# A hybrid decoder layer on one core: the first unit of the merge taken into the last chain of gated linear attention, that branch's constants loaded later, and the last stores issued from two queues

## The chip, the cores and the metric

The kernel runs on one core of one Trainium2 chip. The metric is the device time of one execution in microseconds (us); lower is better. Three runs of the kernel before were timed, and one more execution was profiled.

## What is computed

One layer for 2048 new tokens and 8 x 8 sample tokens, all in f32. The reference, cut to what matters:

```python
z = jnp.einsum('btd,dn->btn', x, w_in)               # all input projections
o_att = swa(q, k, v)                                  # sliding-window attention
o_gla, S = gla(gq, gk, gv, log_a, s0)                 # gated linear attention (GLA), 4 heads
h_att = einsum(o_att * silu(g_att), w_pa)             # merge: four products ...
h_gla = einsum(o_gla * silu(g_gla), w_pg)
merged = sigmoid(x @ w_ra) * h_att + sigmoid(x @ w_rg) * h_gla
x = layer_norm(DN_ALPHA * x + merged @ w_o, ln_g, ln_b)
```

## The kernel before

All large products run on TensorE with each f32 operand split in a high and a low half: `split` (L114) lets ScalarE (ACT) cast the high half and VectorE (DVE) subtract for the low one, and each product takes three matmuls (hi x hi, hi x lo, lo x hi). TensorE's order is the order of the code. The instructions of ACT, DVE, GpSimd (POOL) and SyncE (SP, the main DMA queue) are put in order by a scheduler when the kernel is built; on the chip each of these engines takes its list strictly in order, and an instruction that waits holds all behind it.

The work goes through four stages. Stage 1 is attention, over six chunks of tokens (the loop `for c, (t0, T) in enumerate(CHUNKS)`). Stage 2 is GLA, four heads times six chunks. The parts of a chunk that follow on each other (`gla_a`, `gla_b`, `gla_norm`, `gla_c`, `gla_store`) are put into a list of steps by `chain` (L870), and `tick` runs one step between two projections, so that their matmuls stand between the projections'. In the last chunk of the last head the chain starts before the two gate projections, and what is left of it after them is run by `drain` (L995), with no projection between. The last step holds the transposition of the sample rows (`gla_c(B, "s", ...)`, L781) and the two stores of the gated rows to DRAM (`gla_store`, L788). In the last chunk these go through POOL's queue, behind the state's store (L881) and the two stores of sample states (L842).

Stage 3 is the merge: four passes (`w_pa`, `w_ra`, `w_rg`, `w_pg`) of seven products each (`ORDER`, Strassen-Winograd), each over three ranges of tokens: 84 units. A unit splits one tile of x (`make_x`, from `raw_x` L1045), and for four column groups p = 0..3 runs its matmuls (L1232 to L1234) into one PSUM tile and empties it (`combine`). In the first pass a unit has 4 x 6 = 24 matmuls. Its first product (i = 1) is emptied by a plain copy on ACT into a tile `a12` (L1072). The weights come through `raw_w` (L1014, tag "ws", 11 slots) and x through tag "xc" (5 slots).

Between stages 2 and 3 the memory of stage 2 is closed and given to stage 3's tiles. A new tile waits only for the old ones that it lies upon. The first `a12` tile lies upon one of the two rows of gates that the last `gla_store` writes out: its first copy waits, in both kernels, for that store's semaphore (DMASW5, which reaches the value waited for with the last store on POOL's queue).

Stage 4 is the output projection and the layer norm (`Rows`, L1260). The last tile has 64 rows (32 of each half), is normed in two halves of columns, and is stored by four DMAs from SP (L1300).

At the start SP loads the first weights and x in pieces, and POOL issues seven loads of constants that only GLA reads (L259), one of 192 KB among them.

Of the kernel before, what the change touches and what calls it, by code (L numbers as in the profile page):

```python
# [13 lines left out]
F32R = mybir.dt.float32r  # L14
# [37 lines left out]
def kernel(ctx, tc, io):  # L52
# [45 lines left out]
    def at(d, fn):  # L98

        while len(side) <= d:  # L100
            side.append([])
        side[d].append(fn)
# [61 lines left out]
    def fetch_x(src, t0, T):  # L164

        return [fetch(src, k, t0, T, unit if k < KT // 2 else xstage) for k in range(KT)]
# [87 lines left out]
    wgv = wg[:, :KT * 16].rearrange("p (k r) -> p k r", r=16)  # L254
    nc.scalar.copy(wgs[:, :, 0:16], wgv)
    nc.vector.tensor_tensor(wgs[:, :, 16:32], wgv, wgs[:, :, 0:16].bitcast(F32), ALU.subtract)
    for t, n in ((cmask, "c_causal"), (smask, "c_scausal"), (bsel, "c_bsel"), (rmask, "c_reset"),
                 (smaskr, "c_sreset"), (nw_h, "norm_w"), (bgk, "b_gk")):
        nc.gpsimd.dma_start(t, io[n])  # L259
    nc.vector.tensor_scalar(nw_h, nw_h, 0.5, None, op0=ALU.mult)  # L260
    nc.gpsimd.memset(mhalf, -0.5)
    for t in a_per + [as_per]:
        nc.gpsimd.memset(t, 0.0)
# [289 lines left out]
    for c, (t0, T) in enumerate(CHUNKS):  # L553
# [42 lines left out]

        step(lambda ps: nc.scalar.copy(vT[:, :T], ps), wt1("v"))
        at(1, vtrans)
        if c == 0:
            setup0()  # L600
            at(1, setup1)
            at(2, setup2)
            at(4, setup3)
# [266 lines left out]
    def chain(B):  # L870
# [18 lines left out]
        else:  # L889
            at(7 if short else 6, lambda B=B: gla_store(B))  # L890

    for h in range(GH):
        W2 = {}
        wcap(16 + 6 * h)
        for c, (t0, T) in enumerate(CHUNKS):
            last = c == len(CHUNKS) - 1
            Tp = T - (NS if last else 0)
            nt = Tp // P
            if c == len(CHUNKS) - 3:
                wcap(min(22 + 6 * h, 34))  # L900
            B = dict(h=h, t0=t0, T=T, Tp=Tp, nt=nt, last=last, wgk=R["wgk"], gin=gin, gv=[], sg=[])

            def wt2(*key):
                if c == 0:
                    W2[key] = wget()
                return W2[key]

            gla_z(B)
            sums = [combine_load(lambda n: wtile(name=n)) for _ in range(2 if c in (1, 2, 3) else 0)]

            def combine():
                if sums:
                    with tc.issue_after(pin["d"].ins):
                        combine_do(*sums.pop(0), nc.vector)

            wv = [wt2("v", 0), wt2("v", 1)]
            for i in range((T + P - 1) // P):
                n = min(P, T - i * P)
                ps = pd()
                if n == P:  # L920
                    proj_t(ps[:, :HV], x, i * P, n, wv, HV)
                    v = ps[:, :HV]
                else:
                    v = unit(name="vs")[:n, :HV]
                    proj_s(ps[:, :HV], v, x, i * P, wv, HV)
                    nc.vector.tensor_tensor(v, v, ps[:n, :HV], ALU.add)
                if i % 2 == 0:
                    gvt = wtile(F32R, "gv").rearrange("p (a b v) -> p a b v", a=2, b=2)
                gh, gl = gvt[:, i % 2, 0], gvt[:, i % 2, 1]
                split(gh[:n], gl[:n], v)  # L930
                if n == NS:
                    nc.scalar.copy(gh[NS:], v)
                    nc.vector.tensor_tensor(gl[NS:], v, gh[:NS].bitcast(F32), ALU.subtract)
                B["gv"].append((gh, gl))
                if last and i < 2:
                    wload()
                tick()
            end = last and h == GH - 1
            xf = None if end else fetch_x(io["xT"], *CHUNKS[(c + 1) % len(CHUNKS)])
            ps = pd()  # L940
            proj(ps[:, :T], wt2("k"), x, T)
            gla_k(B, ps[:, :T])
            combine()
            if len(CHUNKS) - 4 < c < len(CHUNKS) - 1:
                wload()
            tick()
            if not last:
                gin = gate_in(h, c + 1)
            elif h + 1 < GH:
                gin = gate_in(h + 1, 0)  # L950
            ps = pd()
            proj(ps[:, :T], wt2("q"), x, T)
            gla_q(B, ps[:, :T])
            tick()
            combine()
            if end:
                chain(B)
            for m in range(2):
                sg = unit(name="sg")
                B["sg"].append(sg)  # L960
                w = wt2("g", m)
                if m == 0 and not end:
                    xn = part_x(xf, samples=(c + 1 == len(CHUNKS) - 1))
                ps = pd()
                proj(ps[:, :T], w, x, T, mid=end)
                gate(sg, ps[:, :T], T)
                if len(CHUNKS) - 4 < c < len(CHUNKS) - 1 and m == 1:
                    wload()
                tick()
            if not end:  # L970
                chain(B)
            x = xn
# [6 lines left out]

    drain()
    phase.close()
    keep, phase, right = ExitStack(), ExitStack(), ExitStack()
    mo = keep.enter_context(tc.tile_pool(name="mo", bufs=1, side="left", reuse_waits="tile"))
# [207 lines left out]
    for tag, n, bufs in (("a12", T, 12), ("fin", T, 6), ("xc", 2 * T, 5), ("ws", KT // 2 * P, 11), ("top", 640, 1),  # L1193
# [1 line left out]
                         ("a21", T, 12), ("cs", 2 * T, 4), ("xh", KT // 2 * T, 2), ("xl", KT // 2 * T, 2),  # L1195
                         ("wh", KT // 2 * P, 8), ("wl", KT // 2 * P, 8)):
        mtile(tag, n, bufs, F32R if tag[1] in "hl" else F32)
    issue_x(0)
    issue_w(-1)
    issue_x(1)  # L1200
    issue_x(2)
    make_x(0)
    make_w(-1)
    issue_w(0)
    wo = []
    for n, (q, i, s) in enumerate(units):
# [12 lines left out]
        issue_w(n + 1)  # L1219
        make_x(n + 1)  # L1220
        make_w(n)
        xh, xl = xp.pop(n)
        for p in range(NP4):
            g = n * NP4 + p
            for j in range(g, g + 4):
                if j not in parts:
                    issue_parts(j)
            wh, wl = wts[n - s, p]
            ps = pa()[:, :T]
            for k in range(q.kh):  # L1230
                ks, ts = slice(k * P, (k + 1) * P), slice(k * T, (k + 1) * T)
                mm(ps, wh[:, ks], xh[:, ts], start=(k == 0), stop=False)  # L1232
                mm(ps, wh[:, ks], xl[:, ts], start=False, stop=False)  # L1233
                mm(ps, wl[:, ks], xh[:, ts], start=False, stop=(k == q.kh - 1))  # L1234
            q.combine(i, p, s, ps, parts.get(g))
            if n == len(units) - 1:
                if p < 3:
                    xr0.append(load_xr(runs(1, p * P, P)))
                x += [part(f, onew) for f in xf[2 * p:2 * p + 2]]
# [20 lines left out]
    class Rows:  # L1260
# [26 lines left out]
        def norm(self):  # L1287
# [6 lines left out]
            for i in range(D // N):  # L1294
                cs = slice(i * N, (i + 1) * N)
                nc.vector.scalar_tensor_tensor(z[:n, cs], z[:n, cs], mv[:n, 0:1], lng[:n, cs],
                                               ALU.subtract, ALU.mult)
                nc.vector.scalar_tensor_tensor(z[:n, cs], z[:n, cs], rs[:n], lnb[:n, cs], ALU.mult, ALU.add)
                for r, o, m in self.runs:
                    nc.sync.dma_start(io["o_y"][r:r + m, cs], z[o:o + m, cs])  # L1300

    HT = NT // 2
    order = [(t, u, n) for t in (1, 0) for u, n in ((0, TM), (TM, TM), (2 * TM, 2 * P))]
# [135 lines left out]
```

## Time and profile before

| what | value |
|---|---|
| three runs | 1843.16, 1848.11, 1849.0 us (median 1848.11) |
| the profiled execution's own time | 1846.22 us |
| its span (first to last instruction) | 1844.4 us |
| TensorE busy | 1807.9 us, 98% of the span |
| DVE, ACT, POOL busy | 69%, 46%, 23% |
| mean granted TensorE clock | 0.992 |

In the profile PE is TensorE's matmuls, PEld its weight loads, SPq and POOLq the issue of DMAs on those queues. A row of a timeline has the start, the time from the first to the end of the last instruction of the row, the engine, the line, the operation with out<-in, how many there are, and in brackets the idle time of the engine before it and what ended it. In a table of stages each engine's busy time stands with its count of instructions, and PEclk is the granted clock (1.00 is full speed).

### The profile page before, as it was taken

What the parts mean: (1) busy time and instruction counts of PE and PEld (TensorE: products, weight loads), DVE (VectorE), ACT (ScalarE), POOL (GpSimd) and SP (SyncE); (2) the same over time, 40 slices, a digit from 0 to 9 for tenths busy, and PEclk for the clock granted to TensorE, in tenths of its full rate; (3) what the DMA queues carried; (4) which work ended last, traced back from release to release, by engine and by line L of the source; (5) the groups of instructions that cost most, each with busy time, mean ns of one, the idle gap of its engine ahead of it and who ended that gap; (6) DMA issues with size and microseconds to landing.
All of it is one profiled execution on the core that took longest, in us unless ns stands there. A gap on an engine that the chain in (4) does not pass through costs nothing.

```text
span 1844.4 us, 32399 instructions
## 1 busy us (share of the span) xinstructions
PE 1807.9 (98%) x11683; PEld 1722.2 (93%) x11683; DVE 1280.9 (69%) x2662; ACT 849.9 (46%) x1947; POOL 422.3 (23%) x559
## 2 busy tenths in 40 slices
PE   8999999999999999999999999999999999989997
PEld 7998988899999999999999999999999999988886
DVE  5677778767776776777667669648657566966655
ACT  5444545645665565656546453435443543211110
POOL 3310111300110111011110243430355153631111
PEclk9999999999999999999999999999999999999998
DMA  7211013534345444543543189858887967895531
GB/s 233 63 56 38 12 47 100 165 131 156 120 148 170 143 143 144 186 132 107 181 145 119 58 274 315 283 178 292 276 311 256 310 216 245 287 312 177 166 111 41
DMA packets 199554, 315.84 MB, mean 171 GB/s; under 512 B 21453, under 2 KB 161189, under 8 KB 199376
## 3 DMA queue, kind: packets, MB, share of 16 engines
q1 hardware_dynamic: 192624, 304.61, 50.5%
q0 software_dynamic: 5616, 7.58, 1.5%
q8 instruction: 92, 1.51, 0.3%
q10 hardware_dynamic: 1152, 1.57, 0.3%
q14 instruction: 70, 0.57, 0.1%
HBM read 228.52 MB, written 86.14 MB: 171 GB/s over the span
## 4 chain that ended last, share of the span: by engine, by line
PE 91%; DVE 3%; DMA 3%; issue 1%; POOL 1%; SPq 0%; ACT 0%; DVEq 0%; ACTq 0%; POOLq 0%
PE pd L185 11%; PE pd L187 11%; PE pd L186 11%; PE pa L1234 9%; PE pa L1233 9%; PE pa L1232 9%; PE pd L199 7%; PE pd L198 7%; PE pd L200 7%; PE pa L421 2%; DMA cs<-tt_d 1%; PE pa L406 1%; PE pa L755 1%; PE pa L753 1%; PE pa L754 1%
## 5 line engine op out<-in xcount | busy, mean ns | idle before, releaser
L185 PE MATMUL pd<-x,wh 128*128 128x384 f32 (+2 forms) x1248 | 409.1, 328 | 7.0 <-ACT x L115 6.3
L186 PE MATMUL pd<-x,wh 128*128 128x384 f32 (+2 forms) x1248 | 403.5, 323 | 0.6 <-DVE x L116 0.3
L187 PE MATMUL pd<-x,wl 128*128 128x384 f32 (+2 forms) x1248 | 403.1, 323 | 0.6 <-DVE wl L116 0.6
L1233 PE MATMUL pa<-xl,wh 128*128 128x352 f32 x1176 | 381.3, 324 | 7.9 <-DVE xl L116 7.6
L1232 PE MATMUL pa<-xh,wh 128*128 128x352 f32 x1176 | 381.4, 324 | 2.6 <-ACT xh L115 2.3
L1234 PE MATMUL pa<-xh,wl 128*128 128x352 f32 x1176 | 381.9, 325 | 0.0
L185 PEld LDWEIGHTS pd<-x,wh 128*128 128x128 f32 x1248 | 236.5, 190 | 17.2 <-issue 8.9
L186 PEld LDWEIGHTS pd<-x,wh 128*128 128x128 f32 x1248 | 236.5, 190 | 2.0 <-DVE x L116 1.5
L187 PEld LDWEIGHTS pd<-x,wl 128*128 128x128 f32 x1248 | 236.1, 189 | 1.0 <-DVE wl L116 1.0
L1233 PEld LDWEIGHTS pa<-xl,wh 128*128 128x128 f32 x1176 | 222.7, 189 | 10.4 <-DVE xl L116 10.1
L1232 PEld LDWEIGHTS pa<-xh,wh 128*128 128x128 f32 x1176 | 222.5, 189 | 3.6 <-ACT xh L115 2.6
L1234 PEld LDWEIGHTS pa<-xh,wl 128*128 128x128 f32 x1176 | 224.5, 191 | 0.0
L116 DVE TENSOR_TENSOR xl<-xs,xh 128x1408 fp32r<-128x1408 f32 x63 | 110.5, 1753 | 69.4 <-ACT xh L115 35.7
L198 PE MATMUL pd<-wh,x 128*128 128x256 f32 x512 | 147.9, 289 | 0.0
L199 PE MATMUL pd<-wh,x 128*128 128x256 f32 x512 | 145.6, 284 | 1.2 <-DVE x L116 1.1
L200 PE MATMUL pd<-wl,x 128*128 128x256 f32 x512 | 144.6, 282 | 0.0
L115 ACT CAST x<-xst 128x384 fp32r<-128x384 f32 (+2 forms) x164 | 78.2, 485 | 139.9 <-PE pd L199 117.9
L115 ACT CAST xh<-xs 128x1408 fp32r<-128x1408 f32 x63 | 86.5, 1372 | 103.9 <-PE pa L1234 81.7
L746 POOL TENSOR_SCALAR sq<-sq 128x1 f32<-128x1 f32 (+1 forms) x68 | 21.4, 314 | 467.2 <-ACT ring L745 467.2
L199 PE MATMUL pd<-woh,x 128*128 128x512 f32 x256 | 101.5, 396 | 0.0
L198 PE MATMUL pd<-woh,x 128*128 128x512 f32 x256 | 101.5, 396 | 0.0
L200 PE MATMUL pd<-wol,x 128*128 128x512 f32 x256 | 101.5, 396 | 0.0
(318 smaller groups left out, 3683.6 us busy)
## 6 DMA issues: line engine op xcount, KB each, us to landing
wst<-wt SPq DMA_DIRECT2D x33, 512.0 KB, 3.6
xs<-xc_d SPq DMA_DIRECT2D x24, 704.0 KB, 5.6
cs<-tt_d SPq DMA_DIRECT2D x48, 352.0 KB, 4.7
u<-xT SPq DMA_DIRECT2D x84, 192.0 KB, 4.0
xst<-xT SPq DMA_DIRECT2D x76, 192.0 KB, 2.6
xs<-xT SPq DMA_DIRECT2D x18, 704.0 KB, 5.9
ws<-w_ra SPq DMA_DIRECT2D x36, 256.0 KB, 4.4
ws<-w_rg SPq DMA_DIRECT2D x36, 256.0 KB, 5.6
```

The lines of the kernel that those rows point to most:

```text
L115: pin["a"] = nc.scalar.copy(dst_h, src)
L116: i = eng.tensor_tensor(dst_l, src, dst_h.bitcast(F32), ALU.subtract)
L185: mm(ps, hi[:, s], xh[:, :T], start=(k == 0), stop=False)
L186: mm(ps, hi[:, s], xl[:, :T], start=False, stop=False)
L187: mm(ps, lo[:, s], xh[:, :T], start=False, stop=(k == n - 1))
L198: mm(ps, xh[:, xs], hi, start=(k == 0), stop=False)
L199: mm(ps, xl[:, xs], hi, start=False, stop=False)
L200: mm(ps, xh[:, xs], lo, start=False, stop=(k == KT - 1))
L421: mm(ot[pr, :], vb[:, pr], A["pT", bi, kv][:, hf], start=(hf == h0), stop=(hf == 1))
L1232: mm(ps, wh[:, ks], xh[:, ts], start=(k == 0), stop=False)
L1233: mm(ps, wh[:, ks], xl[:, ts], start=False, stop=False)
L1234: mm(ps, wl[:, ks], xh[:, ts], start=False, stop=(k == q.kh - 1))
```

## The change

Three edits.

1. The first unit of the merge (pass `w_pa`, i = 1, first range: 24 matmuls) is no longer run by the merge loop. `early_load` loads its x (352 KB) and all its weights (512 KB, one tile) before the k projection of the last chunk; `early_split` splits them after the q projection; `early_product(p)` runs the six matmuls of one column group. Group 0 stands after the last gate projection, group 1 after all steps of the chain but the last, groups 2 and 3 after the last step. They are written to two kinds of PSUM tiles (`pd` for 0 to 2, `pa` for 3). The merge loop then loads no x for unit 0, runs no matmul for it, and only empties the four tiles (`combine`, the copies into `a12`).
2. The seven constants of GLA and the multiplication of `nw_h` come in the third chunk of attention, on POOL behind a copy of that chunk.
3. Of the last tile's four stores, two are issued by ACT.

```diff
+    def gla_constants():
+        for t, n in ((cmask, "c_causal"), (smask, "c_scausal"), (bsel, "c_bsel"), (rmask, "c_reset"),
+                     (smaskr, "c_sreset"), (nw_h, "norm_w"), (bgk, "b_gk")):
+            nc.gpsimd.dma_start(t, io[n])
+        nc.vector.tensor_scalar(nw_h, nw_h, 0.5, None, op0=ALU.mult)
...
+        if c == 2:
+            with tc.issue_after(pin["k"].ins):
+                gla_constants()
...
+    def early_load():
+        r = [wtile(name=n) for n in ("mx", "mw")]
+        nc.sync.dma_start(r[0][:, :2 * MT].rearrange("p (k t) -> p k t", k=2), ua_d[:, :2, :MT])
+        nc.sync.dma_start(r[1].rearrange("q (p c) -> q p c", p=4), io["w_pa"][0, 0].rearrange("p q c -> q p c"))
+        early["raw"] = r
+
+    def early_split():
+        for n_, r, w_ in zip("xw", early.pop("raw"), (2 * MT, D)):
+            hl = wtile(F32R, "mh"), wtile(F32R, "ml")
+            split(hl[0][:, :w_], hl[1][:, :w_], r[:, :w_])
+            early[n_] = hl
+
+    def early_product(p):
+        ps = early[p] = (pd if p < 3 else pa)()[:, :MT]
+        (xh, xl), (wh, wl) = early["x"], early["w"]
+        for k in range(2):
+            ks, ts = slice((2 * p + k) * P, (2 * p + k + 1) * P), slice(k * MT, (k + 1) * MT)
+            mm(ps, wh[:, ks], xh[:, ts], start=(k == 0), stop=False)
+            mm(ps, wh[:, ks], xl[:, ts], start=False, stop=False)
+            mm(ps, wl[:, ks], xh[:, ts], start=False, stop=(k == 1))
...
+            if end:
+                early_load()
...
             if end:
+                early_split()
                 chain(B)
...
+                if end and m == 1:
+                    early_product(0)
                 tick()
...
+    while len(side) > 1:
+        tick()
+    early_product(1)
     drain()
+    early_product(2)
+    early_product(3)
...
-    issue_x(0)
+    issue_x(1)
     issue_w(-1)
-    issue_x(1)
     issue_x(2)
-    make_x(0)
...
-            ps = pa()[:, :T]
-            for k in range(q.kh):
+            ps = pa()[:, :T] if n else early.pop(p)
+            for k in range(q.kh if n else 0):
...
-                for r, o, m in self.runs:
-                    nc.sync.dma_start(io["o_y"][r:r + m, cs], z[o:o + m, cs])
+                for j, (r, o, m) in enumerate(self.runs):
+                    (nc.scalar if self.end and j else nc.sync).dma_start(io["o_y"][r:r + m, cs], z[o:o + m, cs])
```

What this does to the engines' lists is seen at three places. Line numbers of the changed kernel differ from those of before (L1112 is the copy that was L1072, L754 was L748, L787 was L781; L918 to L920 are the early products' matmuls).

The first place is TensorE's list at the end of the chain. Before, from the transpositions of the last block (128 wide) and of the sample rows (64 wide) into unit 0:

```order
L837 MATMUL pa<-gv,kz 128x256
L781 MATMUL pa<-ident,ring 128x128 x2
L781 MATMUL pa<-ident,ring 128x64 x2
L1232 MATMUL pa<-xh,wh 128x352
L1233 MATMUL pa<-xl,wh 128x352
L1234 MATMUL pa<-xh,wl 128x352
```

The same place in the changed kernel, to the first product after the last transposition:

```order
L843 MATMUL pa<-gv,kz 128x256
L787 MATMUL pa<-ident,ring 128x128 x2
L918 MATMUL pd<-mh 128x352
L919 MATMUL pd<-ml,mh 128x352
L920 MATMUL pd<-mh,ml 128x352
L918 MATMUL pd<-mh 128x352
L919 MATMUL pd<-ml,mh 128x352
L920 MATMUL pd<-mh,ml 128x352
L787 MATMUL pa<-ident,ring 128x64 x2
L918 MATMUL pd<-mh 128x352
L919 MATMUL pd<-ml,mh 128x352
```

Group 1 stands behind the 128-wide transpositions and ahead of the 64-wide ones; groups 2 and 3 follow, and then unit 1.

The second place is ACT's list from the last step of the norm of the sample rows into the merge; xh and wh are the high halves of x and of the weights, "a" is the tile a12, and the brackets name the semaphores that an instruction waits for. Before:

```order
L748 ACTIVATE ring<-pa,sq 64x256 [waits Activation_49,Pool_49]
L115 CAST xh<-xc 128x704 [waits DMAHW2_49]
L115 CAST wh<-ws 128x256 [waits DMAHW3_49]
L115 CAST wh<-ws 128x256 [waits DMAHW4_49]
L115 CAST wh<-ws 128x256 [waits DMAHW5_49,PE_49]
L115 CAST wh<-ws 128x256 [waits DMAHW6_49]
L115 CAST xh<-xc 128x704 [waits DMAHW7_49]
L1072 COPY a_13651<-pa 128x352 [waits DMASW2_49,DMASW5_49,DVE_49,PE_49]
```

In the changed kernel:

```order
L754 ACTIVATE ring<-pa,sq 64x256 [waits Activation_49,Pool_49]
L1112 COPY a_13678<-pd 128x352 [waits DMASW5_49,DMASW2_49,DVE_49]
L1112 COPY a_13680<-pd 128x352 [waits DMAHW7_49,PE_49]
L1112 COPY a_13682<-pd 128x352 [waits PE_49]
L1112 COPY a_13684<-pa 128x352 [waits PE_49]
L115 CAST xh<-xc 128x704 [waits DMAHW4_49]
L115 CAST wh<-ws 128x256 [waits DMAHW5_49]
L115 CAST wh<-ws 128x256 [waits DMAHW6_49]
L115 CAST wh<-ws 128x256 [waits DMAHW7_49]
```

The four copies of unit 0 have moved from behind the casts of units 0 and 1 to the front of them; the wait for DMASW5 moved with the first.

The third place is SP's list at the same join. In the changed kernel:

```order
L904 DMA mw<-w_pa 128x4x256
L794 DMA ug_d<-sg 128x256 x2
L1085 DMA xc<-ua_d 128x2x352
L1054 DMA ws<-w_pa 128x256 x4
L1085 DMA xc<-ua_d 128x2x352
L1054 DMA ws<-w_pa 128x256 x2
L1085 DMA xc<-ua_d 128x2x352
L1054 DMA ws<-w_pa 128x256
L1085 DMA xc<-ua_d 128x2x352
L1054 DMA ws<-w_pa 128x256
L1085 DMA xc<-ua_d 128x2x352
L1054 DMA ws<-w_pa 128x256 x4
```

The early loads stand before the last stores of the chunk before (L794); five loads of x (units 1 to 5) and eleven of weights fill all slots, and of the last row's four loads of weights the fourth is the first that waits for a slot.

More of the change, by code (lines that the diff above doesn't have):

```diff
@@ L256 @@
     nc.vector.tensor_tensor(wgs[:, :, 16:32], wgv, wgs[:, :, 0:16].bitcast(F32), ALU.subtract)
[L257 to L260, printed above, removed]
+    def gla_constants():
[3 more added lines that the diff above has]
+        nc.vector.tensor_scalar(nw_h, nw_h, 0.5, None, op0=ALU.mult)
     nc.gpsimd.memset(mhalf, -0.5)
@@ L890, in chain @@
             at(7 if short else 6, lambda B=B: gla_store(B))
+    early = {}
+    def early_load():
[16 more added lines that the diff above has]
+            mm(ps, wl[:, ks], xh[:, ts], start=False, stop=(k == 1))
     for h in range(GH):
@@ L1221 @@
         make_w(n)
-        xh, xl = xp.pop(n)
+        xh, xl = xp.pop(n) if n else (None, None)
         for p in range(NP4):
```

## The prediction

> **What bounds the kernel now.** I read the page first, then the table of what TensorE waited for, the table of stages, and then the timelines of the stages in which it waits.
>
> ```profile
> PE 1807.9 (98%) x11683; PEld 1722.2 (93%) x11683; DVE 1280.9 (69%) x2662; ACT 849.9 (46%) x1947; POOL 422.3 (23%) x559
> PE pa L1233 <- DVE xl L116: 7.6, 5, 2.6
> core 0: us, PE busy (x) PEld busy (x) DVE busy (x) ACT busy (x) POOL busy (x), PEclk, DMA share, GB/s
> 0.00:30.00 30.00, 22.21 (x105) 19.61 (x106) 17.70 (x29) 17.00 (x29) 8.36 (x25) 1.00 0.61 190
> 1052.60:1064.00 11.40, 7.65 (x51) 5.45 (x52) 7.26 (x20) 5.29 (x15) 4.95 (x9) 0.93 0.96 314
> 1831.90:1844.40 12.50, 0.00 (x0) 0.00 (x0) 4.64 (x10) 0.37 (x1) 0.92 (x1) 0.58 0.08 22
> ```
>
> TensorE is busy in 1807.9 of 1844.4 us, so the kernel is as long as TensorE's list plus the 36.5 us in which it waits. Three stages hold most of those: 7.8 us in the first 30, 3.75 us at the join of GLA and merge (11.40 less 7.65), and the 12.5 us after its last matmul. The change works on these three. At the join, TensorE's timeline shows each wait (the row of 7.6 us in five waits above has the last of them), and the table of stages the clock:
>
> ```profile
> 1053.49 0.38 PE L753 MATMUL pa<-st,qih 128*128 128x256 f32 x1 [0.89 <-ACT st L115]
> 1060.71 0.70 PE L781 MATMUL pa<-ident,ring 128*128 128x128 f32 x4 [0.98 <-ACT ring L748]
> 1061.69 0.43 PE L1232 MATMUL pa<-xh,wh 128*128 128x352 f32 x1 [0.27 <-ACT wh L115]
> 1063.54 0.66 PE L1233 MATMUL pa<-xl,wh 128*128 128x352 f32 x1 [1.43 <-DVE xl L116]
> 1064.63 0.49 PE L1233 MATMUL pa<-xl,wh 128*128 128x352 f32 x1
> 1064.92 0.49 PE L1234 MATMUL pa<-xh,wl 128*128 128x352 f32 x1
> 1069.97 0.32 PE L1232 MATMUL pa<-xh,wh 128*128 128x352 f32 x1
> 1070.13 0.32 PE L1233 MATMUL pa<-xl,wh 128*128 128x352 f32 x1
> 1062.47:1069.29 6.82, 5.75 (x19) 5.70 (x20) 3.16 (x8) 0.76 (x2) 1.46 (x3) 0.50 1.03 360
> 1069.29:1076.00 6.71, 6.71 (x43) 6.71 (x43) 4.30 (x6) 6.02 (x17) 2.94 (x3) 1.00 0.48 155
> ```
>
> The waits are 0.89, 0.98, 0.27 and 1.43 us. The last two rows show a second cost: with these waits the clock is granted at 0.50 for 6.82 us. Matmuls of 352 columns start every 0.29 us there (1064.63 to 1064.92) and every 0.16 us at full clock (1069.97 to 1070.13). Unit 1 begins at 1069.97.
>
> **The change: the last stores.** SP's timeline, then the issues of that line and their landing:
>
> ```profile
> 1836.17 1.74 SPq L1300 DMA_DIRECT2D o_y<-z  x4
> L1300 SPq DMA_DIRECT2D o_y<-z x4: 331/385/429, 1836.2 to 1837.5; - x4
> DMA to landing us min/median/max: 1.6/1.7/1.7
> ```
>
> Four issues of about 0.4 us end at 1837.9, the last starting at 1837.5 and the third some 0.45 us before it, behind the second half of z. With two queues the last pair starts together at about 1837.0: -0.45 us, between -0.6 and 0 (if an issue on ACT is slower than on SP).
>
> **The constants.** Rows of ACT, TensorE, the stage from 5 to 11 us, two of the seven loads, and POOL in the third chunk:
>
> ```profile
> 13.83 1.05 ACT L115 CAST wh<-wst 128x1024 fp32r<-128x1024 f32 x1 [0.82 <-DMA wst<-wt]
> 14.93 0.44 PE L185 MATMUL pd<-x,wh 128*128 128x384 f32 x1 [0.66 <-ACT wh L115]
> 5.00:11.00 6.00, 4.77 (x12) 3.64 (x13) 3.50 (x8) 3.21 (x8) 4.35 (x14) 1.00 0.98 312
> rmask<-c_reset POOLq DMA_DIRECT2D x1, 192.0 KB, 5.3
> cmask<-c_causal POOLq DMA_DIRECT2D x1, 64.0 KB, 3.3
> 127.74 1.17 POOL L352 CAST win<-kl 128x128 fp32r<-128x128 f32 x2
> 137.99 0.29 POOL L353 CAST win<-kl 128x128 fp32r<-128x128 f32 x1 [9.08 <-DVE kl L343]
> ```
>
> From 5 to 11 us the DMA engines are full (0.98, 312 GB/s), and TensorE waits at 14.93 for weights that landed at 13.83. The seven constants, 311 KB of which these two rows are 256, take 1.0 us of that rate. I take -0.8 us; bounds -1.0 and 0, if the weights are held by SP's order instead. In the third chunk POOL issues them behind the copies that end at 128.9 and ahead of the one at 137.99, before which it waits 9.08 us for DVE. Seven issues at 0.55 us (two gates' stores take 1.09 in the next fence) end at 132.8 and delay nothing; the product with `nw_h` on DVE stands later still, behind the chunk's first scores. That costs 0.
>
> **The early unit.** Its 24 matmuls are moved, none is added. ACT's, DVE's, SP's and POOL's rows at the join, and the time to landing of POOL's last stores (first one alone, then both):
>
> ```profile
> 1028.70 23.87 SPq L788 DMA_DIRECT2D ug_d<-sg  x4
> 1041.92 0.49 DVE L724 SCALAR_TENSOR_TENSOR dm<-pd,dm 128x320 f32<-128x320 f32 x1 [2.37 <-PE pd L187]
> 1042.78 0.41 ACT L115 CAST qih<-gb 128x256 fp32r<-128x256 f32 x1 [2.30 <-DVE gb L724]
> 1060.56 0.77 ACT L115 CAST xh<-xc 128x704 fp32r<-128x704 f32 x1
> 1061.23 1.32 ACT L115 CAST wh<-ws 128x256 fp32r<-128x256 f32 x4
> 1069.98 0.45 ACT L1072 COPY a<-pa 128x352 f32<-128x352 f32 x1 [6.75 <-PE pa L1233]
> 1073.61 1.20 ACT L1072 COPY a<-pa 128x352 f32<-128x352 f32 x3
> 1062.61 0.88 DVE L116 TENSOR_TENSOR xl<-xc,xh 128x704 fp32r<-128x704 f32 x1
> 1063.94 1.14 SPq L1014 DMA_DIRECT2D ws<-w_pa  x1
> 1060.43 0.86 POOL L842 DMA_DIRECT2D o_ss<-S  x1 [0.27 <-DMA ws<-w_pa]
> 1062.84 1.09 POOL L788 DMA_DIRECT2D ug_d<-sg  x2
> ug_d<-sg POOLq DMA_DIRECT2D x1, 160.0 KB, 5.0
> ug_d<-sg POOLq DMA_DIRECT2D x2, 160.0 KB, 5.8
> ```
>
> The added splits take 0.77 and 0.88 us (x) and 1.05 and, scaled from 0.88 by 1024/704, 1.3 us (weights). They stand where ACT waits 2.30 us for DVE and DVE 2.37 us for TensorE; their loads go out on SP after the second of the four stores from 1028.70, some 8 us ahead. I take 0, at most +0.7 us, if the weights' subtraction pushes `dm` back.
>
> Group 0 (6 x 0.16 = 1.0 us) fills the 0.89 us wait: cost 0. Group 1 doesn't fill the 0.98 us: it stands behind the 128-wide transpositions, and these are what waits at 1060.71, because the PSUM tile they write is the one that the norm of the sample rows is still read from. So that gap stays; group 1 follows from 1061.05 to 1062.05, then the sample transpositions, and groups 2 and 3 end at about 1064.3 (later if the clock drops again at 1062.47; what comes after doesn't depend on it).
>
> What comes after is unit 1, and it needs ACT's cast of its x. On this step the forecast rests. Before, the first copy into `a12` comes at 1069.98, after ACT stood still for 6.75 us. The row blames TensorE, but unit 0's first product was complete when its sixth matmul ended, at 1065.4. The built program has the copy wait for the last store on POOL's queue. That one is the second of the two in the 1062.84 row, issued at 1063.38; 5.0 us for the first and 5.8 as the middle of both make 6.5 for it: it lands at 1069.9, just when the copy runs. Before, this cost nothing: ACT had cast x and weights of units 0 and 1 ahead of the copy, and TensorE had unit 0 to work on. In the changed kernel the four copies stand ahead of all these casts. Queued behind the waiting copy is the x of unit 1, and TensorE, with nothing else left, waits for that.
>
> When does the store land now? Its source is ready after the sample transpositions, some 0.4 us later; POOL is busy until then with the stores ahead of it, so the issue stays at 1063.4. Ahead of it lie the same two stores of 512 KB. SP has sent eleven loads of weights by then, not eight (0.4 MB more), and sends none of those that went out from 1063.94 on (some 0.5 MB). I take 1069.4. The lower bound is 1066.7: from 1061.3, the end of the first store's issue, 1.38 MB at the 360 GB/s of this stage (3.8 us), and 1.6 us, the shortest landing above. The upper is 1070.2, 0.3 later than before.
>
> From landing to unit 1's second matmul: 0.1 to the first copy, 4 copies at 0.37 (three took 1.20), 0.77 for xh, 0.88 for xl and 0.1 between them make 3.3 us. So this matmul comes at 1072.7 where it came at 1070.13: +2.6 us, between -0.1 and +3.4. TensorE has been idle from 1064.3 then, over 7 us, and starts slow. An event of 6.82 us at half clock costs 3.4 us if matmuls fill it, 1.7 if half of it falls in the wait; I take 2.5. (Before, unit 0 ran in such an event; that is contained in the 1070.13 from which I count.) The Trainium skill ("TensorE: Matmul & The Clock Gate", Part 1) has the clock return after some 3.4 us of sustained work; by that the loss would be 1.7 us, and the sum 0.8 us less. The event in the trace is twice as long.
>
> The early unit in all: +2.6 + 2.5 = **+5.1 us**, between +1.6 and +6.8 (+0.7 more if the splits delay).
>
> **Sum.** +5.1 - 0.8 - 0.45 = +3.85 us on the profiled execution's 1846.2, so 1850.1. The median of the runs, 1848.1, is 1.9 above that execution; on its scale the forecast is **1852.0 us**, +0.2%. Its own bounds are 1848.1 (+1.6 - 1.0 - 0.6) to 1855.6 (+6.8 + 0.7).
>
> **Rivals**, on the same scale.
>
> *The gaps are filled and ACT isn't held* (chance 0.10). If the store landed by 1064.3, the last copy would end at 1064.75, a little after group 3, and unit 1's second matmul come at 1064.75 + 0.77 + 0.88 = 1066.4: -3.7 us, of which up to 2.5 is lost again to the clock. With the other edits that is -5.0 to -2.5: 1843.1 to 1845.6. Against it stand 5.0 and 6.5 us of landing; for it, that no row of the profile names the store as what the copy waited for.
>
> *The store lands early* (0.07). The two took long because they stood behind 1 MB. If the queue is emptied sooner, the landing comes 1.7 us (as for the last stores) and 0.3 us for the data after the issue's end at 1063.9: 1065.9. Unit 1's second matmul is then at 1069.2, -0.9; the wait of some 4 us still drops the clock, +1.7; with the rest -0.45: 1847.7. The Trainium skill ("DMA: Bandwidth & Descriptors", Anatomy of one DMA) has a transfer take 2.0 us plus its bytes at 436 GB/s, 2.4 us for 160 KB, which speaks for this. Both stores in the trace took twice as long.
>
> *The weights fall behind, and it is clearly slower* (0.20).
>
> ```profile
> 1096.46 1.26 POOL L1024 TENSOR_TENSOR ws<-ws 128x256 f32<-128x256 f32 x1
> ```
>
> Slots of "ws" come free when DVE has split unit 1's weights. The load that went out at 1063.94 now waits until about 1073, 9 us later, while TensorE's need of it moves by 5.1. The weights that POOL combines lose 4 us of slack; the last of product 6 are combined until 1097.7 (the row), for matmuls near 1104. If less than 4 us is there, TensorE stops in units 6 to 11; the price is up to 4.0: +5.1 + 4.0 - 1.25 = +7.9, 1856.0. For it speaks how close that row is to its use, with a cast and a subtraction still between; against it, that this is one place in many, and later loads wait for TensorE's own pace.
>
> The rest, 0.05, is a half-clock event more or fewer elsewhere (3.4 us each).
>
> **How the numbers follow.** The forecast has 0.58. About 0.3% (5.5 us) is what a measurement of this kernel tells from no change: 1842.6 to 1853.7. Faster than that needs the first rival at its end and an event fewer: 0.05. Slower: the third rival, and the upper part of the forecast's own range: 0.28. Within: 0.67. The range of 1845.5 to 1857.0 holds the forecast's bounds and the second and third rivals, and leaves out most of the first.
>
> **What would show it.** In the changed kernel's profile: ACT idle for some 8 us before the first L1112, which starts within 0.2 us of the last gate store's landing; then four copies, xh, and TensorE's first L1271 about 3.2 us after that start, following an idle of over 6 us; the 0.98 us before L787 unchanged; no wait at group 0; at the start, the second projection's first matmul about 0.8 us earlier. I am wrong if L1112 begins by 1066, or if TensorE waits less than 4 us between its last early product and unit 1.

## The result and the profile after

| | median us | runs | lowest to highest |
|---|---|---|---|
| before | 1847.57 | 10 | 1840.9 to 1849.49 |
| changed | 1855.26 | 10 | 1847.99 to 1859.46 |

The ratio is 1.0048, with a 95% interval of 1.0031 to 1.0064: the changed kernel is slower by 0.48%, some 8.9 us. The forecast was 1852.0 us, +3.85, and a range of 1845.5 to 1857.0, so sign and range held and the size was under half of what came. The range held at its upper side: the bounds that the forecast works out for itself end at +7.5 us, and the time is nearer to the third rival's 1856.0 than to the forecast. A time above 1853.7 had been given a chance of 0.28, against 0.67 for one that can't be told from no change. One execution of all those timed for this document, among the twelve of e7 below, took 4105 us and is left out of its ratio. The profiled execution of the changed kernel is the quickest of its ten: 1847.99 us, with a span of 1846.2, 1.8 above that of before.

The step on which the forecast rested is in this trace as it was forecast, within 0.7 us. ScalarE's timeline at the join (start, duration, line, and in brackets the idle time ahead and what ended it):

```profile
1052.42 0.43 ACT L220 ACTIVATE th<-pd 128x320 f32<-128x320 f32 x1
1059.92 0.47 ACT L754 ACTIVATE ring<-pa,sq 64x256 f32<-64x256 f32 x1 [0.98 <-POOL sq L753]
1070.06 1.16 ACT L1112 COPY a<-pd 128x352 f32<-128x352 f32 x3 [9.67 <-DMA ug_d<-sg]
1071.09 0.48 ACT L1112 COPY a<-pa 128x352 f32<-128x352 f32 x1
1071.43 0.81 ACT L115 CAST xh<-xc 128x704 fp32r<-128x704 f32 x1
```

ScalarE stands still for 9.67 us, and the profile now names what it waited for, the store of the gates (`ug_d<-sg`). Before, the row of this copy blamed TensorE. Behind it come the four copies, and only then the cast of unit 1's x. POOL's issue of the two stores, and their landing from the answer on the tile `sg`:

```profile
1062.73 1.09 POOL L794 DMA_DIRECT2D ug_d<-sg  x2 [0.16 <-DVE sg L790]
DMA to landing us min/median/max: 6.7/6.8/6.8
```

The second store lands at 1069.95, 0.1 us ahead of the copy. TensorE's timeline at the same place, and the table of stages around the half clock:

```profile
1053.76 0.39 PE L760 MATMUL pa<-st,qih 128*128 128x256 f32 x1 [0.18 <-DVE st L116]
1060.44 0.44 PE L787 MATMUL pa<-ident,ring 128*128 128x128 f32 x2 [1.00 <-ACT ring L754]
1063.92 0.32 PE L920 MATMUL pa<-mh,ml 128*128 128x352 f32 x1
1072.60 0.66 PE L1270 MATMUL pa<-xh,wh 128*128 128x352 f32 x1 [8.37 <-ACT wh L115]
1073.22 0.66 PE L1271 MATMUL pa<-xl,wh 128*128 128x352 f32 x1
core 0: us, PE busy (x) PEld busy (x) DVE busy (x) ACT busy (x) POOL busy (x), PEclk, DMA share, GB/s
1067.09:1077.33 10.24, 4.73 (x15) 4.34 (x16) 4.15 (x8) 5.58 (x14) 0.96 (x2) 0.50 0.28 91
1077.33:1084.00 6.67, 6.67 (x44) 6.67 (x43) 2.44 (x5) 4.89 (x13) 0.74 (x1) 1.00 0.23 72
```

The 0.89 us wait ahead of group 0's place is gone, the wait ahead of the 128-wide transpositions is still 1.00 us, the last early product begins at 1063.92, and then TensorE has nothing to do for 8.37 us. When unit 1 comes, the clock is at 0.50 until 1077.33. Unit 2 begins 26.46 us after ScalarE's last tanh of a gate (the 1052.42 row), and in the kernel before 21.13 us after it (that tanh is at 1052.71 there): the join costs **+5.3 us**, where +5.1 was forecast.

The other two edits gave nothing. At the start, TensorE's and ScalarE's rows of before, then of after:

```profile
28.46 0.49 PE L594 MATMUL pa<-ident,vT 128*128 128x128 f32 x3
28.79 1.05 ACT L115 CAST wh<-wst 128x1024 fp32r<-128x1024 f32 x1 [2.23 <-DMA wst<-wt]
31.41 0.51 PE L301 MATMUL pa<-oh,rbh 33*128 33x384 f32 x1 [0.84 <-ACT brow L306]
```

```profile
27.41 0.49 PE L597 MATMUL pa<-ident,vT 128*128 128x128 f32 x3
28.91 1.05 ACT L115 CAST wh<-wst 128x1024 fp32r<-128x1024 f32 x1 [2.72 <-DMA wst<-wt]
31.51 0.44 PE L304 MATMUL pa<-oh,rbh 33*128 33x384 f32 x1 [2.00 <-ACT brow L309]
```

TensorE is 1.05 us ahead at the transposition of vT, but the next weights land no earlier (the cast that waits for them is at 28.91, and was at 28.79), the copies of the bias rows stand behind that cast on ScalarE, and TensorE waits 2.00 us for them where it waited 0.84.

At the end, the instructions of the last line (the program's close), before and after:

```profile
L1425 POOLq DRAIN  x3: 46/106/9372, 1834.3 to 1844.2; - x3
L1425 SPq DRAIN  x3: 7/7/7, 1839.3 to 1843.9; - x3
```

```profile
L1463 POOLq DRAIN  x3: 46/98/9371, 1836.0 to 1845.9; - x3
L1463 SPq DRAIN  x3: 7/7/7, 1840.7 to 1845.7; - x3
1836.07 0.92 POOL L1330 TENSOR_TENSOR rs<-rs,mhalf 64x1 f32<-64x1 f32 x1 [6.47 <-DVE rs L1329]
1837.94 1.03 ACTq L1338 DMA_DIRECT2D o_y<-z  x2
```

In the kernel before, VectorE's last addition into `rs` is at 1834.0 and SP is through with the last landing at 1839.3, 5.3 us later; in the changed kernel these are 1835.8 and 1840.7, 4.9 us apart: the last store did land 0.44 us sooner. But POOL's last instruction is followed by a drain of 9.37 us, and the program ends 0.8 us behind that in both kernels: 10.43 us from the addition to the end, with one queue or two. The rows of before showed this already.

### The profile page after: what moved, and what is told of

It reads as the page before. It is cut to its first block, busy times and chain, and to the rows that moved or that the text cites. A ratio compares the mean times of both kernels' runs of the same rounds, so it can differ in the third digit from the quotient of the medians.

```text
span 1846.2 us, 32397 instructions
## 1 busy us (share of the span) xinstructions
PE 1805.9 (98%) x11683; PEld 1719.1 (93%) x11683; DVE 1277.0 (69%) x2663; ACT 851.6 (46%) x1948; POOL 421.4 (23%) x559
## 4 chain that ended last, share of the span: by engine, by line
PE 89%; DVE 4%; DMA 3%; ACT 1%; issue 1%; POOL 1%; SPq 0%; DVEq 0%; ACTq 0%; POOLq 0%
PE pd L185 10%; PE pd L187 10%; PE pd L186 10%; PE pa L1271 8%; PE pa L1270 8%; PE pa L1272 8%; PE pd L199 7%; PE pd L200 7%; PE pd L198 7%; PE pa L424 2%; DMA cs<-tt_d 1%; PE pa L409 1%; PE pa L760 1%; PE pa L761 1%; PE pa L759 1%
## 5 line engine op out<-in xcount | busy, mean ns | idle before, releaser
L1271 PE MATMUL pa<-xl,wh 128*128 128x352 f32 x1168 | 377.0, 323 | 6.3 <-DVE xl L116 6.1
L1272 PE MATMUL pa<-xh,wl 128*128 128x352 f32 x1168 | 376.2, 322 | 0.0
L1272 PEld LDWEIGHTS pa<-xh,wl 128*128 128x128 f32 x1168 | 220.1, 188 | 0.1
```

## The experiments

One theory: ScalarE's queue stands behind a copy whose memory the last store still reads, and this hold is the cost. Its rivals: that the price lies elsewhere (constants, stores, weights), that other waits would take the hold's place, or that it is the waiting itself and not the queue behind it. All runs were timed beside the kernel before on the same chip. "Below" and "above" are against it.

**e1 and e10, the early unit alone** (constants and stores as before), and **e9, the changed kernel again** beside e10.

> The changed kernel with the constants and the last stores as before: the early unit alone. Theory (ScalarE is held until the last gate store lands): ScalarE idle for 8 to 10 us before the first copy of unit 0, TensorE idle for about 8.4 us before unit 1, then half clock; matmuls of unit 2 and after stand about 5.3 us later than in the kernel before, and the time is 0.2 to 0.5% above it (+4 to +9 us), most of what the whole change costs. Rival (the cost lies in the other two edits, or in the weights behind): within 0.1% of the kernel before.

> The changed kernel once more, beside e10 and e11 on one chip. The first timing gave 0.48% (0.31 to 0.64) above the kernel before, the early unit alone 0.30% (0.17 to 0.44). Theory (the early unit's hold is the whole cost, 5.3 us in the trace, and the other two edits are worth nothing): 0.2 to 0.4% above the kernel before, and within 0.1% of e10. Rival (constants and stores add to it): 0.45% or more, and over 0.15% above e10.

> The early unit alone once more, as in e1: 0.2 to 0.4% above the kernel before by the theory, and the same as e9; by the rival 0.15% or more below e9.

e1 gave 1.0030 (1.0017 to 1.0044), e10 1.0039 (1.0024 to 1.0054), e9 1.0043 (1.0027 to 1.0059). e9 is a little above the 0.2 to 0.4% that was expected, and it is 0.04% from e10. The early unit alone and the whole change differ by less than the intervals: the unit is the cost. Rows of ScalarE and TensorE in e1:

```profile
1067.38 1.16 ACT L1106 COPY a<-pd 128x352 f32<-128x352 f32 x3 [8.45 <-DMA ug_d<-sg]
1069.93 0.66 PE L1264 MATMUL pa<-xh,wh 128*128 128x352 f32 x1 [7.16 <-ACT wh L115]
```

**e2, the constants alone.**

> The kernel before with GLA's constants loaded in the third chunk, nothing else. Theory from the two traces (the microsecond gained in the first 28 us is given back at the next weights, which land no earlier): TensorE reaches the first products with the identity about 1 us earlier, waits about 1.2 us longer at the bias products near 31 us, and everything from 40 us on stands within 0.3 us of the kernel before; the time is unchanged within 0.15%. Rival (the gain of 0.8 us of the prediction holds): all from 40 us on 0.8 us earlier.

1.0002 (0.9987 to 1.0016): no change, but the interval is some 2.5 us to either side, so the time alone can't tell 0.8 us from nothing, and the rows have to. TensorE reaches the identity products at 27.51 (27.41 in the changed kernel, 28.46 before), and waits 1.47 us for the bias rows (0.84 before). One number of the theory missed: the trace stood not within 0.3 us of before from 40 us on but 1.2 us later. In it the half clock that follows these waits lasts 10.24 us, and 6.83 before (rows of before, then of e2):

```profile
31.64:38.47 6.83, 6.83 (x22) 5.86 (x22) 5.70 (x11) 3.00 (x5) 1.44 (x3) 0.50 0.87 297
```

```profile
31.09:41.33 10.24, 10.24 (x31) 9.35 (x32) 5.90 (x11) 3.14 (x5) 4.18 (x8) 0.50 0.90 281
```

TensorE's 120th matmul is still 0.2 us ahead of before, and its 150th, behind the stretch, is 1.2 us late. The other traces with the constants moved have 3.41 or 6.83 us here. The last tanh of the gates lies between 1049.6 and 1053.4 in the fourteen profiled executions, with both settings of the constants at either end, so a single trace can't show an edit of this size in this stage.

**e11, the last stores from two queues alone.**

> The kernel before with the last stores from two queues, nothing else. Theory (POOL's drain of 9.37 us ends last): the last store lands about 0.44 us sooner after the last rows' statistics, POOL's drain ends where it did, and the span's end stands 10.4 us after the last addition to the variance, as in the kernel before; the time is the same within 0.15%. Rival (the prediction's -0.45 us holds): 9.9 us.

1.0005 (0.9990 to 1.0020), too wide an interval for 0.45 us; the rows have 10.43 us from the addition into `rs` to the end, as by the theory, though the last store lands 0.3 us sooner.

**e3, the same order of work, other memory under the copies.** Two entries of the list that lays out the merge's tiles are swapped, so that `a12` lies where no late store reads:

```diff
-    for tag, n, bufs in (("a12", T, 12), ("fin", T, 6), ("xc", 2 * T, 5), ...
+    for tag, n, bufs in (("fin", T, 6), ("a12", T, 12), ("xc", 2 * T, 5), ...
```

> The changed kernel with two entries of the list that lays out the merge's tiles swapped (fin ahead of a12), so that the first copies write memory that the last gate stores don't read. The order of the work is the same. Theory (the held copy is the cost): ScalarE's first copy of unit 0 runs by 1064, unit 1's x is cast by 1066, TensorE idles about 2.3 us instead of 8.4 before unit 1; unit 2 and after stand 5 to 9 us earlier than in the changed kernel, and the time is 0 to 4 us below the kernel before. Rival (the wait is only passed on: the weights, or the x of unit 1, or a fin tile that now waits for the store, are next): TensorE still idles over 6 us in units 1 to 4, and the time stays 4 us or more above the kernel before.

```profile
1057.45 0.43 ACT L1112 COPY a<-pd 128x352 f32<-128x352 f32 x1
1062.91 0.43 PE L1270 MATMUL pa<-xh,wh 128*128 128x352 f32 x1 [1.52 <-ACT wh L115]
```

The first copy runs 7.9 us after the last tanh, not 17.6, TensorE idles 1.52 us, and unit 2 comes 6.9 us earlier than in the changed kernel. The ratio is 1.0001 (0.9985 to 1.0017): the whole loss is gone with the wait. The hold is shown. That the time would fall below the kernel before did not come: unit 2 comes only 0.5 to 1.5 us earlier than in the kernels without the early unit.

**e5, the same memory, another order on ScalarE.** Unit 0's copies are issued behind the casts of the next x and weights:

```diff
-                nc.scalar.copy(a, ps)
+                if s == 0 and self is passes[0]:
+                    with tc.issue_after(pin["a"].ins):
+                        nc.scalar.copy(a, ps)
+                else:
+                    nc.scalar.copy(a, ps)
```

> The changed kernel, with the copies of the first units put behind the casts of the next x and weights on ScalarE's queue. The first copy still writes the memory that the last gate store reads. Theory (what costs is not the wait itself but what is queued behind it): the first copy still starts at the store's landing, at about 1070, but TensorE begins unit 1 within 1 us of the last early product; it then stops for 2 to 4 us before unit 2, whose accumulator needs the fourth copy. Unit 2 begins 0 to 2.5 us earlier than in the kernel before, and the time is within 0.15% of it. Rival (unit 1 is held by something else too, its weights or the memory of its x): TensorE idles over 6 us before unit 1 as in the changed kernel, and the time is 4 us or more above the kernel before.

```profile
1068.46 1.17 ACT L1114 COPY a<-pd 128x352 f32<-128x352 f32 x3 [6.95 <-DMA ug_d<-sg]
1070.03 0.43 PE L1274 MATMUL pa<-xh,wh 128*128 128x352 f32 x1 [4.07 <-ACT a L1114]
```

The copy waits for the store as long as ever, and unit 1 begins 11.6 us after the last tanh instead of 20.2. TensorE then stops for 4.07 us ahead of unit 2, for the fourth copy. 1.0008 (0.9996 to 1.0020). So a wait of nearly 7 us on ScalarE costs little when what TensorE needs stands ahead of it, and 5 us when it stands behind.

**e12, the stores from ScalarE's queue**, where they don't stand behind the 1 MB of the state:

```diff
-            (nc.gpsimd if B["last"] and B["h"] == GH - 1 else nc.sync).dma_start(
+            (nc.scalar if B["last"] and B["h"] == GH - 1 else nc.sync).dma_start(
```

> The changed kernel, with the two last gate stores issued from ScalarE's queue in place of POOL's: the copy still waits for the store, but on POOL's queue the stores stood behind the two stores of the state and took 6.8 us to land, while the loads from SP's queue in that stage took 5.1 to 5.6. Theory (the price is the landing, us for us): the copies start where the stores land, 1 to 4 us earlier than in the changed kernel, unit 2 begins as much earlier (within 1 us, as the half clock ends on a grid of 3.4 us), and the time is 0.05 to 0.25% above the kernel before. Rival (ScalarE is held by another wait just as long, the stores of the state): the copies start where they did, at 10 us and more after the last norm of ScalarE, and the time is 0.3% or more above.

```profile
1066.84 1.17 ACT L1112 COPY a<-pd 128x352 f32<-128x352 f32 x3 [6.59 <-DMA ug_d<-sg]
1069.39 0.66 PE L1270 MATMUL pa<-xh,wh 128*128 128x352 f32 x1 [5.29 <-ACT wh L115]
```

The stores now land 4.1 us after their issue, 6.8 in the changed kernel (the answer on the tile `sg`):

```profile
DMA to landing us min/median/max: 4.0/4.1/4.2
```

The copies start 3.1 us earlier after the tanh than in the changed kernel, unit 1 too, and unit 2 3.4 us: microsecond for microsecond, as the theory says. The time, 1.0030 (1.0019 to 1.0042), is above the 0.05 to 0.25% that was expected and at the rival's 0.3%; the rows decide for the theory, as the rival had the copies start where they did.

**e6, both mends and the second early product ahead of the last 128-wide transpositions** (`while len(side) > 2` for `> 1`).

> The changed kernel with the tiles laid out as in e3, the copies behind the casts as in e5, and the second early product one step earlier, ahead of the last 128-wide transpositions. Theory (nothing else stands in the way): the 0.98 us wait before those transpositions is filled, TensorE idles under 0.5 us before unit 1, and unit 2 begins 4 to 6 us earlier than in the kernel before; the time is 0.15 to 0.35% below it. Rival (the waits come back at unit 2 or 3, at a copy that waits for the stores of the state, or the clock drops all the same for 6.8 us): under 2 us are left at unit 4, and the time is the same within 0.1%.

```profile
1063.70 1.14 ACT L1114 COPY a<-pd 128x352 f32<-128x352 f32 x3
1072.37 0.43 PE L1275 MATMUL pa<-xl,wh 128*128 128x352 f32 x1 [0.81 <-DVE xl L116]
```

From the last tanh to unit 2 TensorE now has no wait but the 0.18 us ahead of L760, the clock does not drop, and unit 2 begins 14.79 us after the tanh, 6.3 us earlier than before. The first wait is 0.81 us, in unit 3. Yet the ratio is 0.9990 (0.9977 to 1.0002), a third of what the join gained, less than the 0.15 to 0.35% that was expected, and not told from no change. Some of the rest shows in the table below (output: 197.0, where the kernels without the early unit have 194.4 to 195.4), and e6's profiled execution has a half-clock stretch from 1514.8 to 1521.6 us that the one of before has not. Where the remainder went is open.

**e4, the last power of -0.5 on other engines**, in the kernel before; **e7**, the same and two queues for the last stores; **e8**, all three parts of the change, e6's mends, and e4 with ScalarE's table fetched ahead (the load of a function table, 1.28 us, that stands ahead of the root in e4; that line is not shown):

```diff
             nc.vector.tensor_scalar(rs[:n], mv[:n, 1:2], 4.0 * EPS, None, op0=ALU.add)
-            nc.gpsimd.tensor_tensor(rs[:n], rs[:n], mhalf[:n], ALU.pow)
+            if self.end:
+                nc.scalar.activation(rs[:n], rs[:n], AF.Sqrt)
+                nc.vector.reciprocal(rs[:n], rs[:n])
+            else:
+                nc.gpsimd.tensor_tensor(rs[:n], rs[:n], mhalf[:n], ALU.pow)
```

> The kernel before, with the power of -0.5 of the last 64 rows done as a square root on ScalarE and a reciprocal on VectorE, not on POOL. In both traces POOL's last instruction is followed by a drain of 9.37 us, which ends 4.3 and 4.75 us after SP has seen the last store land. Theory (POOL's drain sets the end, so that earlier stores are worth nothing): POOL's drain begins some 6 us earlier, SP's last landing is next, the span ends about 5.5 to 6 us after the last issue of a store, not 7, and the time falls by 3 to 4.3 us. Rival (the drain waits for the last stores, or has its length from what else is under way, and ends 4 to 5 us after the landing in any case): no change, within 0.5 us in the tail.

> e4 and the last stores from two queues. Theory (with POOL's drain out of the way the last landing sets the end): the span ends 0.4 to 0.5 us sooner after the last row's end on VectorE than in e4, which was 3.37 us after the last group of z ended there; the time is 0.45 us below e4, too little for the runs to tell. Rival (something else ends the span): the same end as e4.

> All three parts of the change, with e6's mends at the join, and the last rows' power as a square root on ScalarE with its table fetched ahead. The theories together: the join as in e6 (4 to 6 us earlier), and the tail 4.1 to 5 us shorter (3.66 us as in e4's trace, 0.45 by the two queues, up to 0.9 by the table fetched ahead): 8 to 11 us below the kernel before, 0.43 to 0.6%. If one of the two is a matter of chance in the profiled run only, half of that.

The close of e4:

```profile
L1429 POOLq DRAIN  x3: 46/102/9904, 1824.2 to 1838.2; - x3
L1429 SPq DRAIN  x3: 7/7/7, 1837.6 to 1837.9; - x3
```

POOL's drain now begins at 1824.2, behind the power of the rows before, and is over when SP has seen the last landing at 1837.6; the program ends 0.9 us later. From the addition into `rs` to the end it is 6.72 us in e4 (10.43 before), 6.41 in e7, 5.78 in e8. e4: 0.9977 (0.9961 to 0.9994), e7: 0.9979 (0.9966 to 0.9991), e8: **0.9957 (0.9941 to 0.9973)**, the quickest version, 1836.31 us. e8 is at the lower edge of what was expected. The two queues are worth 0.31 us once POOL is out of the way, and nothing while its drain ends last.

All profiled executions side by side, in us, worked out from the rows of their traces. The columns: from ScalarE's last tanh of a gate to the first copy into `a12`, to unit 1's and unit 2's first matmul; from the merge's thirtieth last matmul to VectorE's last addition into `rs`; and from there to the end.

| | first copy | unit 1 | unit 2 | output | close |
|---|---|---|---|---|---|
| before | 17.3 | 17.26 | 21.13 | 194.4 | 10.43 |
| e2 constants | 15.9 | 16.35 | 20.16 | 194.4 | 10.42 |
| e4, e7 power moved | 16.7, 16.3 | 16.22, 16.36 | 20.13, 20.17 | 195.2, 195.4 | 6.72, 6.41 |
| e11 stores | 17.7 | 16.11 | 21.13 | 195.1 | 10.43 |
| changed, e9 | 17.6, 17.3 | 20.18, 19.86 | 26.46, 25.97 | 194.6, 197.0 | 10.43, 10.42 |
| e1, e10 early unit | 16.4, 16.6 | 18.97, 19.10 | 25.87, 25.45 | 199.6, 198.7 | 10.43, 10.43 |
| e12 stores on ACT | 14.6 | 17.11 | 23.09 | 195.6 | 10.27 |
| e3 other memory | 7.9 | 13.33 | 19.61 | 195.6 | 10.42 |
| e5 casts first | 18.1 | 11.64 | 19.69 | 195.3 | 10.43 |
| e6 both | 11.1 | 10.71 | 14.79 | 197.0 | 10.43 |
| e8 all | 11.1 | 10.71 | 14.79 | 196.3 | 5.78 |

In the five executions with the copies at the head of ScalarE's queue behind the store (the changed kernel, e9, e1, e10, e12), unit 1 follows the first copy by 2.55 us each time. In the first four of them unit 2 comes at 25.9 on average, and at 20.5 in the five without the early unit: the hold, with the half clock behind it, costs 5.4 us.

## Why the prediction was right in the main, and where it was not

**The hold: right.** "ACT held until the store lands": the first copy at 1070.06 (forecast 1069.4, upper bound 1070.2), 0.1 us behind the landing. From the landing to unit 1's second matmul 3.27 us (forecast 3.3). The landing was taken too early, though: that matmul comes 20.80 us after the last tanh and came 17.42 before, +3.4 us where +2.6 was taken and +3.4 was the upper bound. e3 takes the wait away and the loss with it; e5 and e12 show that the price is what is queued behind the copy, and follows the landing.

**Group 0 and group 1: right.** The 0.89 us wait is filled, the 0.98 us one stays (1.00), and e6, which moves group 1 ahead of the transpositions, fills it. The splits cost nothing, as forecast: they push `dm` back by 0.8 us (it begins 10.0 us ahead of the last tanh, 10.8 before), and TensorE waits for nothing there.

**The clock: right in size, in part by luck.** From unit 1's first matmul to unit 2 it is 6.28 us in the changed kernel and 3.87 before, a loss of 2.4 (forecast 2.5). Counted from unit 1's second matmul, as the forecast counts, it is 2.0. The event lasted 10.24 us, not 6.82, but over half of it fell into the wait. So +3.4 and +2.0 stand where +2.6 and +2.5 were taken: the join's sum is closer, +5.3 for +5.1, than its terms. The Trainium skill ("TensorE: Matmul & The Clock Gate", Part 1) has the clock come back after at least one busy window of about 3.4 us, and the window run free of the kernel. The traces agree: in the five executions in which unit 1 began at half clock (the changed kernel, e9, e1, e10, e12), full speed came back 4.0 to 6.1 us after unit 1's start, always over one window and under two.

**The constants: wrong.** "I take -0.8 us; bounds -1.0 and 0, if the weights are held by SP's order instead." It was the second bound. The 0.8 us were seen at one wait and taken for the whole stage; the same stage has a later wait for weights, 14 us on, which the earlier start doesn't move (28.79 and 28.91).

**The last stores: wrong.** "-0.45 us, between -0.6 and 0" was worked out for the landing, and the landing did come 0.44 us sooner. That the landing ends the program was never shown. POOL's drain, 9372 ns in the close of before, ends last. Together these two steps had taken 1.25 us off the sum: without them the forecast's own terms give +5.1, 0.28%.

**What was not in the sum.** The runs put the early unit at +0.30 and +0.39%, the whole change at +0.48 and +0.43%: 5.5 to 8.9 us. The join accounts for 5.4. The output column shows where more went in single traces: 194.4 to 195.4 in the five kernels without the early unit, but 197.0, 199.6 and 198.7 in three of the four executions with the full hold, and 197.0 and 196.3 in e6 and e8 (195.3 to 195.6 in e3, e5 and e12). TensorE waits there for the last two loads of w_o. In e9 the rows are

```profile
1670.24 0.50 PE L198 MATMUL pd<-woh,x 128*128 128x512 f32 x1 [1.16 <-ACT woh L115]
1671.50 0.50 PE L200 MATMUL pd<-wol,x 128*128 128x512 f32 x1 [0.53 <-DVE wol L116]
```

and the trace of before has no wait at this place. In e1 and e10 such waits are followed by a half-clock stretch that the other traces don't have, in e1:

```profile
1669.92:1673.33 3.41, 3.34 (x8) 2.70 (x9) 1.81 (x4) 0.00 (x0) 0.00 (x0) 0.50 0.12 46
```

At half speed this costs about 1.7 us more (an estimate: half of 3.41). The changed kernel's first profile happens to have neither, which is one reason why it shows +1.8 us only. The last of the loads lands 21.0 to 22.7 us after the merge's last matmul in these five traces, and 18.5 to 20.3 us in the other nine. Why is open: no run was made for it, e9 has the program of the changed kernel, and it is not shown that the early unit is the cause. The third rival (weights behind in units 6 to 11, up to 4 us) did not come in that form: TensorE waits 1.1 us between 1080 and 1200 us before, 1.0 in the changed kernel, and 2.1 to 2.8 in e1, e9 and e10, mostly for x and not for weights; e11, without the early unit, has 2.8 too.

**The other rivals.** That ACT isn't held (0.10) and that the store lands early (0.07) are refuted by the 1070.06 row. e3 is the first of them made true, and gave 1.0001 where the rival had put -5.0 to -2.5 us: of its terms the -1.25 was not there, and the join's gain, 1.5 us against before, is within its -3.7 to -1.2 and too small for the runs to tell.

## What to carry to other kernels

When work is moved ahead on one engine, look at what its results are written into: a copy into memory that a late store still reads can be harmless at the end of a queue and cost microsecond for microsecond at its head. Either other memory (one swapped entry in a list) or another order on the waiting queue takes the price away; which semaphore the copy waits on is in the built program, while a profile in which the wait is hidden can name the wrong engine, as the row of before did. Before a saving at the end of a kernel is priced, find which engine's close ends last, and before one at the start, look for the next wait of the same kind behind it.

## What the hardware did that was not expected

**POOL's drain.** After POOL's last instruction its drain goes on for 8.45 us: 9.37 us with a power of 0.92 us in it (before and after), 9.90 with one of 1.46 (e4); in e12 it is 9.22 with 0.92, so 8.3 us. It sets the end of these programs unless POOL's last instruction ends some 8.5 us ahead of the last landing, as in e4, e7 and e8.

**The pace of the merge differs from execution to execution.** In the stage from 1180 to 1430 us TensorE is busy all the time at full clock, and yet its count of matmuls differs. The same stage of before, of the changed kernel, of e1 and of e10, from the tables of stages:

```profile
1180.00:1430.00 250.00, 250.00 (x1565) 250.00 (x1564) 170.01 (x241) 115.84 (x183) 86.82 (x68) 1.00 0.79 266
```

```profile
1180.00:1430.00 250.00, 250.00 (x1575) 250.00 (x1575) 169.80 (x244) 116.10 (x184) 89.86 (x70) 1.00 0.79 267
```

```profile
1180.00:1430.00 250.00, 250.00 (x1576) 250.00 (x1575) 169.41 (x243) 116.28 (x184) 92.63 (x70) 1.00 0.78 267
```

```profile
1180.00:1430.00 250.00, 250.00 (x1553) 250.00 (x1553) 167.24 (x238) 113.49 (x181) 87.21 (x68) 1.00 0.79 266
```

The mean spacing of the matmuls' starts is 160.0, 158.9, 158.9 and 161.1 ns. In all fourteen traces it is one of these three for hundreds of microseconds on end, or passes from one to another. e1 and e10 are one program, timed on the same chip, so it is neither the kernel's nor the chip's doing. Over the merge's 3504 matmuls one such step of 1.11 ns is 3.9 us, about half of the spread of the runs (1840.9 to 1849.5 before). What picks the pace is open.

**The half-clock stretches differ in length too.** They are 3.41, 6.83 or 10.24 us long in all fourteen traces, up to the last matmul, and one place can have one or the other. At waits of up to 2.6 us in the merge's last units there are 6.83 us in the trace of before and 3.41 in that of the changed kernel:

```profile
1632.49:1639.32 6.83, 4.69 (x16) 4.69 (x17) 6.68 (x10) 3.59 (x9) 2.74 (x4) 0.50 0.98 312
```

```profile
1637.11:1640.53 3.42, 3.42 (x14) 3.42 (x13) 3.29 (x6) 1.29 (x3) 1.88 (x2) 0.50 1.06 390
```

e4 and e7, the same program up to the last stores, have 3.41 and 6.83 us there. From unit 2 to the merge's last matmul the profiled execution of before takes 570.35 us and the changed kernel's 566.90, so 3.4 us of its join's 5.3 come back: some 2.2 by the quicker pace (159.4 ns on average for 160.0, outside the waits and the half clock), the rest by shorter waits and the shorter stretch. Pace and stretches differ as much between executions of one program, so this is put down to chance and not to the change, and one profiled execution of each kernel can't show a difference of a few microseconds.
